# A hybrid decoder layer on one core: modulation weights transposed and summed along rows, streamed weights laid out in order of use

## The chip, the cores and the metric

One core of a Trainium2 chip runs one program, written in the Tile framework, which orders the instructions of each engine when the program is built. The metric is the device time of one execution in microseconds (us).

## The reference

One layer with two sub-layers works on x, 256 tokens by 2048 channels, in float32. All weights come from HBM, and each is used once.

```python
c_act = silu(c)                                              # c: (1, 2048)
mod = (c_act @ w_ada + b_ada).reshape(6, 2048)               # w_ada: (2048, 12288)
shift1, scale1, gate1, shift2, scale2, gate2 = mod
h = rms_norm(x, norm_g[0]) * (1 + scale1) + shift1
proj = h @ w_in                                              # w_in: (2048, 10288)
...                                                          # pooling, gated MLP and attention mixers
y = merged @ w_out                                           # merged: sigmoid gates * (mixer @ w_br_*)
x = x + gate1 * rms_norm(y, norm_g[1])
h = rms_norm(x, norm_g[2]) * (1 + scale2) + shift2
y = relu(h @ w_ff1)**2 @ w_ff2                               # 2048 -> 8192 -> 2048
x = x + gate2 * rms_norm(y, norm_g[3])
```

The product with w_ada is a matrix times one vector. It reads 100.7 MB, more than a quarter of all bytes, and does little arithmetic with them.

## The kernel before

Every large product goes through one pattern. `load_raw` issues one DMA on SP's queue for four (in the early phases two to four) k-tiles of 128 rows by 512 columns into a ring of three `raw` buffers of 1 MB. `split` makes a high part on ACT (`whi`, L183) and the rest on DVE (`wlo`, L184), two k-tiles at a time, in rings of three buffers each. `mm_a` then issues three matmuls on PE (TensorE) per k-tile and half of the tokens: high by high, low by high, high by low (L203 to L205). With 512 columns per tile of weights the DMA reads runs of 2 KB, since the weights lie in HBM row by row.

The early part runs in five phases over k (`PH`: 2, 3, 4, 3 and 4 k-tiles). In each phase twelve blocks of 512 columns of w_in are multiplied; their sums stay in PSUM or are added to SBUF by `evict`, on DVE (L396, L398). A phase can begin only when `modulate` has applied scale1 and shift1 for its k-tiles, so the modulation for phase n+1 is computed during phase n, by a Python generator that is stepped between the blocks (`step`). Behind the phases come the attention, the branch products and the gates, w_out, a normalisation, and then the feed-forward part, the longest. In all of these `fill` steps other generators (`side`) beside each 1 MB of weights: `"ada"` holds the modulation for the second sub-layer and the gates.

The modulation before has k on the partitions. `ada_gemv` loads about 1 MB of w_ada, by two DMAs for two sections of columns that lie apart or by one where they are adjacent, and multiplies it on DVE by the column `sil` of silu(c), accumulating over k-tiles into `acc` (L281, L283). What is left is a sum over the 128 partitions, which PE does. `ada_cols` needs the result per channel on the partitions: it multiplies each 128x128 piece of `acc` as stationary operand by one column of ones (L292; the trace shows two matmul records for each of these f32 matmuls), then adds the bias and the norm weight (L296 to L298). `ada_row` needs the result as a row repeated on all partitions (`gg1`, `gg2`): it splits `acc`, multiplies by `ones_r` (L313, L314) and combines with broadcast loads of b_ada and norm_g.

At the start SP's queue carries in order: c (8 KB), the identity, the first part of w_ada, the four parts of x (512 KB each), the rest of w_ada for phase 0, then w_in.

Of the kernel before, what the change touches and what calls it, by code (L numbers as in the profile page):

```python
# [13 lines left out]
P = 128  # L14
S = 256
# [30 lines left out]
V_END = 160  # L46
# [3 lines left out]
def trunk_kernel(ctx: ExitStack, tc: tile.TileContext, consts, x, c, norm_g, w_ada, b_ada, w_in,  # L50
                 pool_w, pool_scale, gmlp_ln_g, gmlp_ln_b, gmlp_ws, gmlp_bs, cmp_pos, cmp_w1,
                 cmp_b1, cmp_w2, cmp_b2, w_br_pool, w_br_gmlp, w_br_nsa, w_out, w_ff1, w_ff2, out):
# [48 lines left out]
    sil = cp.tile([P, KT], F32, name="sil")  # L101
    a_col = cp.tile([P, KT], F32, name="a_col")
    t_col = cp.tile([P, KT], F32, name="t_col")
    a2_col = cp.tile([P, KT], F32, name="a2_col")
# [8 lines left out]
    crow = pre.tile([KT, P], F32, name="crow")  # L113
    rows0 = pre.tile([96, P], F32, name="rows0")
    rows1 = pre.tile([64, P], F32, name="rows1")
    nc.sync.dma_start(crow, c.rearrange("o (r p) -> (o r) p", p=P))
# [26 lines left out]
    def load_cols():
        A.activation(ones_r, ones, AF.Copy)
        tp1 = bank("x")
        T.transpose(tp1[:, 0:V_POS + 32], rows0[0:V_POS + 32], ident[0:V_POS + 32, 0:V_POS + 32])
        T.transpose(tp1[:, V_BADA:V_END], rows1, ident[0:64, 0:64])
# [21 lines left out]
    def load_raw(src):  # L169
        k, n = src.shape[1], src.shape[2]  # L170
        raw = st.tile([P, 2048], F32, name="raw", tag="raw", bufs=3)
        v = raw[:, 0:k * n].rearrange("p (k n) -> p k n", n=n)
        nc.sync.dma_start(v, src)
        return v
# [11 lines left out]

    def kview(w):
        return w[0].rearrange("(kt p) n -> p kt n", p=P)

    win_v, wada_v = kview(w_in), kview(w_ada)  # L190
    brp_v, brg_v, brn_v = kview(w_br_pool), kview(w_br_gmlp), kview(w_br_nsa)
    wout_v, ff1_v, ff2_v = kview(w_out), kview(w_ff1), kview(w_ff2)

# [52 lines left out]
    def gemm_a_last(wv, c0, act, stores, row0=0):  # L246
# [3 lines left out]
        for u in range(0, KT, 4):  # L250
            raw = load_raw(wv[:, row0 + u:row0 + u + 4, c0:c0 + 512])
# [13 lines left out]
    def ada_gemv(c0, c1, acc):  # L265

        n = acc.shape[2]
        nk = 1024 // n
        for u in range(0, KT, nk):
            raw = ring[0].tile([P, 2048], F32, name="raw", tag="raw", bufs=ring[1])[:, 0:2 * nk * n]  # L270
            if c1 == c0 + n:
                rv = raw.rearrange("p (k s n) -> p s k n", k=nk, s=2)
                nc.sync.dma_start(raw.rearrange("p (k n) -> p k n", k=nk), wada_v[:, u:u + nk, c0:c0 + 2 * n])
            else:
                rv = raw.rearrange("p (s k n) -> p s k n", k=nk, s=2)
                for s_, c_ in enumerate((c0, c1)):
                    nc.sync.dma_start(rv[:, s_], wada_v[:, u:u + nk, c_:c_ + n])
            for k in range(nk):
                kt = u + k
                if kt == 0:  # L280
                    V.tensor_scalar(acc, rv[:, :, k], sil[:, 0:1], None, ALU.mult)  # L281
                else:
                    V.scalar_tensor_tensor(acc, rv[:, :, k], sil[:, kt:kt + 1], acc, ALU.mult, ALU.add)  # L283
            yield

    def ada_cols(k0, nk, sec, vsec, vg, a_c, t_c):

        acc = ad.tile([P, 1024], F32, name="acc", tag="acc", bufs=2)[:, 0:256 * nk]
        yield from ada_gemv(sec * D + k0 * P, (sec + 1) * D + k0 * P, acc.rearrange("p (s n) -> p s n", s=2))
# [6 lines left out]
        V.tensor_add(a_c[:, ks], ps[:, nk:2 * nk], cols[:, bs + KT:bs + KT + nk])  # L296
        V.scalar_tensor_tensor(a_c[:, ks], a_c[:, ks], 1.0, cols[:, vg + k0:vg + k0 + nk], ALU.add, ALU.mult)
        V.tensor_add(t_c[:, ks], ps[:, 0:nk], cols[:, bs:bs + nk])  # L298

    def ada_row(n, sec, gi, gg):  # L300

        acc = ad.tile([P, 1024], F32, name="acc", tag="acc", bufs=2)
        c0 = sec * D + n * 1024
        gs = gg[:, n * 1024:(n + 1) * 1024]
        nc.sync.dma_start(gs, b_ada[0, c0:c0 + 1024].partition_broadcast(P))
        yield from ada_gemv(c0, c0 + 512, acc.rearrange("p (s n) -> p s n", s=2))
        hv, lv = split(acc.rearrange("p (k n) -> p k n", k=2))
        for b in range(2):
            ps = bank("pv")
            bs = slice(b * 512, (b + 1) * 512)  # L310
            gb = ad.tile([P, 512], F32, name="gb", tag="gb", bufs=1)
            nc.sync.dma_start(gb, norm_g[0, gi, n * 1024 + b * 512:n * 1024 + (b + 1) * 512].partition_broadcast(P))
            T.matmul(ps, ones_r, hv[:, b], start=True, stop=False)  # L313
            T.matmul(ps, ones_r, lv[:, b], start=False, stop=True)  # L314
            V.tensor_add(gs[:, bs], gs[:, bs], ps)
            V.tensor_mul(gs[:, bs], gs[:, bs], gb)
# [18 lines left out]
    PH = ((0, 2), (2, 3), (5, 4), (9, 3), (12, 4))  # L335
# [37 lines left out]
    Q0, KV0, NG0, BG0 = 1536, 2560, 4096, 4144  # L373

    def part(pool, tag, bufs=1):
# [6 lines left out]
    early = [(0, pool_p, None), (512, u_p, None), (1024, v_p, None),  # L382
             (KV0, kc_p, None), (KV0 + 512, ks_p, None), (KV0 + 1024, kw_p, None),
             (Q0, flat(q32[:, 0:4]), -0.125), (Q0 + 512, flat(q32[:, 4:8]), -0.125)]
    early += [(BG0 + b * D + n * 512, dst, None) for (b, n), dst in g_p.items()]
# [3 lines left out]
    def evict(e):  # L389
        _, dst, scale = early[e]  # L390
# [297 lines left out]
    early_steps = []  # L688
    for kc in range(4):
        side["ada"][0].append(ada_cols(4 * kc, 4, 3, 2, V_G2, a2_col, t2_col))  # L690
    for ph, (k0, nk) in enumerate(PH):
# [9 lines left out]
        if ph < NP - 1:  # L701
            nxt, ns = [ada_cols(*PH[ph + 1], 0, 0, V_G0, a_col, t_col)], KT // (8 // PH[ph + 1][1])
# [3 lines left out]
        for i, e in enumerate(order):  # L706
# [7 lines left out]
            c0, _, _ = early[e]  # L714
# [3 lines left out]
            raw = load_raw(win_v[:, k0:k0 + nk, c0:c0 + 512])  # L718
# [23 lines left out]
    raw = load_raw(win_v[:, :, NG0:NG0 + 48])  # L742
# [5 lines left out]
    gT = ad.tile([48, S], F32, name="gT", tag="gb", bufs=1)  # L748
# [12 lines left out]
    def gate_chunk(b, n):  # L761
        ps = gemm(win_v, BG0 + b * D + n * 512, act)
# [39 lines left out]
    def row(n, *args):  # L802
        yield from ada_row(n, *args)
        rows.append(n)
# [192 lines left out]
```

## Time and profile before

| what | value |
|---|---|
| median of 3 runs | 1546.1 us (1539.91 to 1547.72) |
| profiled execution, own time | 1540.46 us |
| its span, first to last instruction | 1537.8 us |
| mean granted clock of PE | 0.981 |
| PE busy in the span | 1472.0 us (96%) |
| DVE busy | 1072.6 us (70%) |
| ACT busy | 764.7 us (50%) |
| moved by DMA | 368.61 MB, mean 240 GB/s |

The profile shows one execution, from its first instruction to its last; the execution's own time has 2.7 us more around it. A share of busy time is a mean over stages that differ: PE at 96% leaves 66 us of the span in which it does nothing, and a clock below 1 stretches its matmuls without making it idle. A chain of waits is read backwards from the last instruction; a row in it says what ended last at that place.

### The profile page before, as it was taken

The page shows a single profiled execution, that of the slowest core. Times are in us where ns is not written, and L with a number is a line of the kernel's source. Part 1 is how long each engine was busy: PE and PEld are TensorE (multiplying, and loading weights), DVE is VectorE, ACT ScalarE, POOL GpSimd, SP SyncE. Part 2 cuts the span into 40 slices and gives each one's busy share as a digit, 9 for nine tenths or more (in the row PEclk, how much of TensorE's full clock was granted, in tenths as well). Part 3 has the DMA queues.
Part 4 walks back from the last instruction along what each step waited for, and adds up shares of the span by engine and source line. Part 5 has one row for each costly group of instructions (what it writes and reads, how often), then busy time and mean ns, then how long its engine had stood idle before and what let it go on. Part 6 is the DMA issues. An engine that isn't in the chain of part 4 may idle for free.

```text
span 1537.8 us, 17519 instructions
## 1 busy us (share of the span) xinstructions
PE 1472.0 (96%) x6635; PEld 1193.9 (78%) x6635; DVE 1072.6 (70%) x1358; ACT 764.7 (50%) x1089; POOL 30.0 (2%) x39
## 2 busy tenths in 40 slices
PE   3989999999999999999989999999999999999997
PEld 2768877887777668787867888888888888888886
DVE  6788898778887787779887556666655445454465
ACT  5644334653677765254456453345433544344542
POOL 1000001002000010000000000000000000000000
PEclk8999998998999999999999999999999999999999
DMA  9998988665566668888975667777676555566553
GB/s 321 316 330 302 324 309 302 212 200 180 197 232 212 223 222 316 298 295 294 338 257 174 215 240 246 228 251 241 220 243 216 184 190 191 192 192 192 184 195 113
DMA packets 182339, 368.61 MB, mean 240 GB/s; under 512 B 9722, under 2 KB 22272, under 8 KB 182000
## 3 DMA queue, kind: packets, MB, share of 16 engines
q1 hardware_dynamic: 180640, 363.30, 69.8%
q0 software_dynamic: 1616, 4.20, 0.9%
q8 instruction: 52, 0.85, 0.2%
q14 instruction: 31, 0.25, 0.0%
HBM read 365.38 MB, written 2.10 MB: 239 GB/s over the span
## 4 chain that ended last, share of the span: by engine, by line
PE 83%; DVE 7%; DMA 5%; ACT 2%; issue 1%; SPq 0%; DVEq 0%; ACTq 0%
PE ps_mm L204 25%; PE ps_mm L205 25%; PE ps_mm L203 25%; DVE wlo L184 3%; DVE acc L283 2%; PE ps_x L360 2%; DMA raw<-in_w_ada_dram 2%; ACT whi L183 1%; DMA raw<-in_w_in_dram 1%; PE ps_x L292 1%; DMA raw<-in_w_out_dram 1%; PE ps_x L637 1%; PE ps_x L671 1%; DMA x_h<-in_x_dram 1%; PE ps_pv L663 1%
## 5 line engine op out<-in xcount | busy, mean ns | idle before, releaser
L184 DVE TENSOR_TENSOR wlo<-raw,whi 128x1024 fp32r<-128x1024 f32 x484 | 577.1, 1199 | 373.3 <-ACT whi L183 372.2
L183 ACT ACTIVATE whi<-raw 128x1024 fp32r<-128x1024 f32 x484 | 499.6, 1037 | 606.2 <-PE ps_mm L205 510.7
L204 PE MATMUL ps_mm<-wlo,hhi 128*128 128x512 f32 x1260 | 500.7, 397 | 9.6 <-DVE wlo L184 9.6
L203 PE MATMUL ps_mm<-whi,hhi 128*128 128x512 f32 x1260 | 497.3, 398 | 9.2 <-ACT whi L183 6.1
L205 PE MATMUL ps_mm<-whi,hlo 128*128 128x512 f32 x1260 | 498.7, 396 | 0.0
L204 PEld LDWEIGHTS ps_mm<-wlo,hhi 128*128 128x128 f32 x1260 | 239.6, 190 | 66.3 <-DVE wlo L184 16.7
L203 PEld LDWEIGHTS ps_mm<-whi,hhi 128*128 128x128 f32 x1260 | 238.5, 190 | 61.8 <-ACT whi L183 8.2
L205 PEld LDWEIGHTS ps_mm<-whi,hlo 128*128 128x128 f32 x1260 | 239.3, 190 | 51.4 <-issue 1.9
L283 DVE SCALAR_TENSOR_TENSOR acc<-raw,sil,acc 128x1024 f32<-128x1024 f32 (+2 forms) x195 | 235.2, 1206 | 7.6 <-DMA raw<-in_w_ada_dram 5.3
L203 PE MATMUL ps_mm<-whi,fhi 128*128 128x512 f32 x496 | 193.3, 390 | 0.0
L205 PE MATMUL ps_mm<-whi,flo 128*128 128x512 f32 x496 | 193.0, 389 | 0.0
L204 PE MATMUL ps_mm<-wlo,fhi 128*128 128x512 f32 x496 | 193.0, 389 | 0.0
L205 PEld LDWEIGHTS ps_mm<-whi,flo 128*128 128x128 f32 x496 | 93.1, 188 | 19.3
L204 PEld LDWEIGHTS ps_mm<-wlo,fhi 128*128 128x128 f32 x496 | 93.1, 188 | 19.3
L203 PEld LDWEIGHTS ps_mm<-whi,fhi 128*128 128x128 f32 x496 | 93.1, 188 | 19.2
L643 ACT ACTIVATE e<-e,m 128x128 f32<-128x128 f32 (+1 forms) x64 | 28.3, 443 | 1.9 <-DVE m L640 1.9
L398 DVE TENSOR_TENSOR part<-part,ps_mm 128x512 f32<-128x512 f32 x40 | 25.9, 681 | 4.4 <-PE ps_mm L205 4.4
L909 ACT ACTIVATE r_t<-ps_mm 128x512 f32<-128x512 f32 x32 | 18.8, 589 | 15.7 <-PE ps_mm L205 15.7
L403 DVE TENSOR_TENSOR pl<-ps_x,ph 128x512 fp32r<-128x512 f32 (+1 forms) x32 | 20.9, 675 | 8.1 <-ACT ph L402 8.1
L653 ACT ACTIVATE e<-e,s 128x128 f32<-128x128 f32 (+1 forms) x64 | 23.1, 441 | 5.5 <-DVE s L650 5.5
L204 PE MATMUL ps_mm<-wlo,qe 128*128 128x512 f32 x64 | 25.0, 390 | 0.0
L203 PE MATMUL ps_mm<-whi,qe 128*128 128x512 f32 x64 | 24.9, 392 | 0.0
(283 smaller groups left out, 1060.3 us busy)
## 6 DMA issues: line engine op xcount, KB each, us to landing
raw<-in_w_ff_dram SPq DMA_DIRECT2D x128, 1024.0 KB, 5.2
raw<-in_w_in_dram SPq DMA_DIRECT2D x56, 1024.0 KB, 5.3
raw<-in_w_ada_dram SPq DMA_DIRECT2D x104, 512.0 KB, 5.5
raw<-in_w_ada_dram SPq DMA_DIRECT2D x32, 1024.0 KB, 5.1
raw<-in_w_in_dram SPq DMA_DIRECT2D x24, 768.0 KB, 5.9
raw<-in_w_out_dram SPq DMA_DIRECT2D x16, 1024.0 KB, 5.3
raw<-in_w_ada_dram SPq DMA_DIRECT2D x32, 384.0 KB, 5.8
raw<-in_w_br_nsa_dram SPq DMA_DIRECT2D x8, 1024.0 KB, 5.7
```

What stands on the lines that cost most here:

```text
L183: A.activation(hv, v, AF.Copy)
L184: V.tensor_sub(lv, v, hv.bitcast(F32))
L203: T.matmul(outs[t], ahi[:, kt, ts_], hv[:, k, c0:c0 + n], start=f, stop=False, skip_group_check=True)
L204: T.matmul(outs[t], ahi[:, kt, ts_], lv[:, k, c0:c0 + n], start=False, stop=False, skip_group_check=True)
L205: T.matmul(outs[t], alo[:, kt, ts_], hv[:, k, c0:c0 + n], start=False, stop=l, skip_group_check=True)
L283: V.scalar_tensor_tensor(acc, rv[:, :, k], sil[:, kt:kt + 1], acc, ALU.mult, ALU.add)
L360: T.transpose(tb[:, (k * NT + t) * P:(k * NT + t + 1) * P], src[t][:, (k2 * 2 + k) * P:(k2 * 2 + k + 1) * P], ident)
L398: V.tensor_add(d, d, ps)
L403: V.tensor_sub(lo, src, hi.bitcast(F32))
L643: A.activation(e[:, br, 0:L], e[:, br, 0:L], AF.Exp, scale=-1.0, bias=m8[:, hh, br:br + 1], accum_out=s8[:, hh, br:br + 1])
L653: A.activation(es[hh][:, br, 0:L], es[hh][:, br, 0:L], AF.Copy, scale=s8[:, hh, br:br + 1])
L909: A.activation(r_t[:, t], ps[t], AF.Relu)
```

## The change

Two things change together.

First, the modulation. The weights come as `w_adaT`, the transpose of w_ada, so that a row holds all 2048 inputs of one output channel. `sil` becomes a 128x2048 tile: c is broadcast to all partitions by two DMAs of 512 KB, and ACT and DVE compute tanh(c/2) and (tanh + 1) * c on it. `ada_col` loads 128 rows of `w_adaT` (1 MB, one DMA, 8 KB for each partition) and one DVE instruction multiplies them by `sil`, scales by 0.5 and sums along the row into one column, `accum_out=col`. `ada_cols` calls it for shift and scale of each k-tile and then only adds bias and norm weight; nothing is left for PE. The gates are columns first (`ada_gate`, 16 calls each); `to_rows` turns them into rows in four steps by multiplying the identity with the column on DVE, splitting that, and two matmuls by `ones_r` on PE. The broadcast loads of b_ada and norm_g fall away; these vectors are transposed with the others at the start. The first gate is now first in the `"ada"` queue, and `to_rows` for it has a queue of its own, `"rows"`.

Second, the layout. All streamed weights are given to the program in another order: each block that one DMA loads is contiguous in HBM, with 8 KB (for 4 k-tiles; 4 or 6 KB in phases with 2 or 3) for each partition. The blocks, the matmuls and the splits stay as they are. The new order is made with the inputs, outside the program.

```diff
-    sil = cp.tile([P, KT], F32, name="sil")
+    sil = ad.tile([P, D], F32, name="sil")
+    for h in range(2):
+        hs = slice(h * 1024, (h + 1) * 1024)
+        nc.sync.dma_start(sil[:, hs], c[0, hs].partition_broadcast(P))
...
+    for h in range(2):
+        hs = slice(h * 1024, (h + 1) * 1024)
+        th = ring[0].tile([P, 2048], F32, name="raw", tag="raw", bufs=ring[1])[:, 0:1024]
+        A.activation(th, sil[:, hs], AF.Tanh, scale=0.5)
+        V.scalar_tensor_tensor(sil[:, hs], th, 1.0, sil[:, hs], ALU.add, ALU.mult)
...
-            raw = load_raw(wv[:, row0 + u:row0 + u + 4, c0:c0 + 512])
+            raw = load_raw(wv[c0, (row0 + u) // 4])
...
-    def ada_gemv(c0, c1, acc):
...
+    def ada_col(col, sec, k):
+
+        raw = ring[0].tile([P, 2048], F32, name="raw", tag="raw", bufs=ring[1])
+        r0 = sec * D + k * P
+        nc.sync.dma_start(raw, w_adaT[r0:r0 + P, :])
+        V.tensor_tensor_reduce(raw, raw, sil, 0.5, 0.0, ALU.mult, ALU.add, accum_out=col)
...
-        ps = bank("x")
-        for k in range(2 * nk):
-            T.matmul(ps[:, k:k + 1], acc[:, k * P:(k + 1) * P], ones[:, 0:1], start=k == 0, stop=k == 2 * nk - 1,
-                     skip_group_check=True)
+        for k in range(k0, k0 + nk):
+            for s_, c_ in enumerate((t_c, a_c)):
+                ada_col(c_[:, k:k + 1], sec + s_, k)
+                yield
...
+    def ada_gate(sec, vb, vg, g_c):
+
+        for k in range(KT):
+            ada_col(g_c[:, k:k + 1], sec, k)
+            yield
+        V.tensor_add(g_c, g_c, cols[:, vb:vb + KT])
+        V.tensor_mul(g_c, g_c, cols[:, vg:vg + KT])
+        gated.append(sec)
...
+    def to_rows(g_c, gg):
+
+        for n in range(4):
+            dh, dl = (st.tile([P, 1024], F32R, name=t, tag=t, bufs=3)[:, 0:512] for t in ("whi", "wlo"))
+            d32 = st.tile([P, 2048], F32, name="raw", tag="raw", bufs=3)[:, 0:512]
+            V.tensor_tensor(d32.rearrange("p (k n) -> p k n", k=4), ident.unsqueeze(1).broadcast_to([P, 4, P]),
+                            g_c[:, 4 * n:4 * n + 4].unsqueeze(2).broadcast_to([P, 4, P]), ALU.mult)
+            A.activation(dh, d32, AF.Copy)
+            V.tensor_sub(dl, d32, dh.bitcast(F32))
+            ps = bank("x")
+            T.matmul(ps, ones_r, dh, start=True, stop=False)
+            T.matmul(ps, ones_r, dl, start=False, stop=True)
+            A.activation(gg[:, n * 512:(n + 1) * 512], ps, AF.Copy)
+            yield
...
-            nxt, ns = [ada_cols(*PH[ph + 1], 0, 0, V_G0, a_col, t_col)], KT // (8 // PH[ph + 1][1])
+            nxt, ns = [ada_cols(*PH[ph + 1], 0, 0, V_G0, a_col, t_col)], 2 * PH[ph + 1][1]
...
-    side["ada"][0][1:1] = [row(n, 2, 1, gg1) for n in range(2)]
+    while 2 not in gated:
+        step(side["ada"][0])
+    side["rows"] = [[to_rows(g1_col, gg1)], 0.5, 0.0]
```

## Rows read from the trace of the kernel before

**Rows 1.** Page, part 1: busy time of each engine over the whole span.
```profile
PE 1472.0 (96%) x6635; PEld 1193.9 (78%) x6635; DVE 1072.6 (70%) x1358; ACT 764.7 (50%) x1089; POOL 30.0 (2%) x39
```

**Rows 2.** Windows: stretch, length, busy us (count) per engine, clock, DMA share, GB/s.
```profile
10.00:20.00 10.00, 2.62 (x10) 1.82 (x11) 7.98 (x21) 8.22 (x14) 0.00 (x0) 1.00 1.06 361
33.00:300.00 267.00, 254.49 (x1116) 206.35 (x1117) 227.09 (x269) 128.25 (x169) 6.71 (x11) 0.97 0.88 303
70.00:120.00 50.00, 44.83 (x191) 35.10 (x190) 44.00 (x50) 21.91 (x29) 0.00 (x0) 1.00 0.93 331
232.00:240.00 8.00, 8.00 (x31) 6.79 (x30) 4.19 (x9) 3.33 (x6) 0.00 (x0) 0.58 0.89 333
300.00:800.00 500.00, 489.46 (x2239) 384.94 (x2238) 403.09 (x624) 278.58 (x493) 16.79 (x11) 0.98 0.73 251
345.00:600.00 255.00, 250.44 (x1146) 188.62 (x1145) 208.59 (x407) 163.17 (x352) 15.89 (x10) 0.97 0.64 218
600.00:690.00 90.00, 86.47 (x384) 70.85 (x383) 66.88 (x65) 38.84 (x46) 0.00 (x0) 0.96 0.87 307
```

**Rows 3.** Chain that ended last, in time order: start us, duration us, what.
```profile
4.79 9.40 DMA x_h<-in_x_dram
...
28.24 1.65 PE ps_x L292 x8
...
63.90 1.25 PE ps_x L292 x12
...
120.06 1.92 PE ps_x L292 x16
...
232.31 2.23 PE ps_x L292 x16
...
397.19 1.68 PE ps_x L292 x16
```

**Rows 4.** Timeline of the start: start us, us, engine, line, operation, idle before.
```profile
24.40 0.27 PE L147 MATMUL ps_x<-cst,rows 64*128 64x64 f32 x1
...
24.99 3.10 DVE L283 SCALAR_TENSOR_TENSOR acc<-raw,sil,acc 128x512 f32<-128x512 f32 x4
...
30.36 1.09 ACT L330 ACTIVATE h<-xnT,t_col,a_col 128x256 f32<-128x256 f32 x2 [4.51 <-DVE a_col L297]
...
32.97 0.79 PE L203 MATMUL ps_mm<-whi,hhi 128*128 128x512 f32 x1 [3.10 <-ACT hhi L331]
```

**Rows 5.** Groups by shape on DVE: count, busy us, mean ns, idle before.
```profile
L283 DVE SCALAR_TENSOR_TENSOR acc<-raw,sil,acc 128x1024 f32<-128x1024 f32 x150 | 193.5, 1290 | 6.3 <-DMA raw<-in_w_ada_dram 4.8
...
L640 DVE CUSTOM_DVE_ANT_0 e<-ps_x,cst 128x256 f32<-128x256 f32 x32 | 11.8, 420 | 1.4 <-PE ps_x L637 1.3
...
L640 DVE CUSTOM_DVE_ANT_0 e<-ps_x,cst 128x128 f32<-128x128 f32 x32 | 7.8, 287 | 1.7 <-PE ps_x L637 1.5
```

**Rows 6.** Timeline of DVE during attention: start us, us, operation.
```profile
508.30 1.28 DVE L283 SCALAR_TENSOR_TENSOR acc<-raw,sil,acc 128x1024 f32<-128x1024 f32 x1
509.50 0.68 DVE L403 TENSOR_TENSOR pl<-ps_x,ph 128x512 fp32r<-128x512 f32 x1
...
516.61 0.42 DVE L640 CUSTOM_DVE_ANT_0 e<-ps_x,cst 128x256 f32<-128x256 f32 x1
...
518.33 0.42 DVE L640 CUSTOM_DVE_ANT_0 e<-ps_x,cst 128x256 f32<-128x256 f32 x1
```

**Rows 7.** Waits of PE: line, released by, total us, times, longest us.
```profile
PE ps_mm L204 <- DVE wlo L184: 9.6, 11, 2.0
PE ps_mm L203 <- ACT whi L183: 6.1, 4, 3.5
...
PE ps_pv L535 <- DVE Gt L531: 3.6, 1, 3.6
```

**Rows 8.** Chain between 200 and 260 us: start us, duration us, what.
```profile
199.91 0.23 PE ps_mm L203
...
235.17 0.43 PE ps_mm L205
```

More of the change, by code (lines that the diff above doesn't have):

```diff
@@ L45, with trunk_kernel @@
 V_BADA = 96
-V_END = 160
+V_G1, V_G3, V_BG1, V_BG2 = 160, 176, 192, 208
+V_END = 224
+Q0, KV0, NG0, BG0 = 1536, 2560, 4096, 4144
+PH = ((0, 2), (2, 3), (5, 4), (9, 3), (12, 4))
+EARLY_G = [(b, n) for n in range(2) for b in range(2)]
+LATE_G = [(b, n) for n in range(2, 4) for b in range(2)] + [(2, n) for n in range(4)]
+EARLY = [0, 512, 1024, KV0, KV0 + 512, KV0 + 1024, Q0, Q0 + 512] + [BG0 + b * D + n * 512 for b, n in EARLY_G]
+LATE = [BG0 + b * D + n * 512 for b, n in LATE_G]
 @with_exitstack
-def trunk_kernel(ctx: ExitStack, tc: tile.TileContext, consts, x, c, norm_g, w_ada, b_ada, w_in,
+def trunk_kernel(ctx: ExitStack, tc: tile.TileContext, consts, w_adaT, win_e, win_g, win_n, brp_v, brg_v, brn_v,
+                 wout_v, ff1_v, ff2_v, x, c, norm_g, b_ada,
                  pool_w, pool_scale, gmlp_ln_g, gmlp_ln_b, gmlp_ws, gmlp_bs, cmp_pos, cmp_w1,
-                 cmp_b1, cmp_w2, cmp_b2, w_br_pool, w_br_gmlp, w_br_nsa, w_out, w_ff1, w_ff2, out):
+                 cmp_b1, cmp_w2, cmp_b2, out):
     nc = tc.nc
@@ L169, in load_raw @@
     def load_raw(src):
[L170 to L174, printed above, removed]
+        n = src.shape[1]
+        raw = st.tile([P, 2048], F32, name="raw", tag="raw", bufs=3)[:, 0:n]
+        nc.sync.dma_start(raw, src)
+        return raw.rearrange("p (k n) -> p k n", n=512) if n % 512 == 0 else raw
     def split(v, store=None, ahead=150):
@@ L262, in gemm_a_last @@
         return ps
-    def ada_gemv(c0, c1, acc):
[L267 to L284, printed above, removed]
@@ L300, in ada_row @@
[L300 to L316, printed above, removed]
+        V.tensor_add(t_c[:, ks], t_c[:, ks], cols[:, bs:bs + nk])
@@ L381, in trunk_kernel @@
     g_p = {(b, n): part(gp, "gt", 4) for n in range(2) for b in range(2)}
[L382 to L385, printed above, removed]
+    early = [(dst, None) for dst in (pool_p, u_p, v_p, kc_p, ks_p, kw_p)]
+    early += [(flat(q32[:, 4 * n:4 * n + 4]), -0.125) for n in range(2)]
+    early += [(g_p[b, n], None) for b, n in EARLY_G]
     NE = len(early)
@@ L389, in evict @@
     def evict(e):
-        _, dst, scale = early[e]
+        dst, scale = early[e]
         for b, ps in enumerate(opened.pop(e)):
@@ L799, in trunk_kernel @@
     gg1 = g1p.tile([P, D], F32, name="gg1")
-    rows = []
-    def row(n, *args):
-        yield from ada_row(n, *args)
-        rows.append(n)
-    side["ada"][0][1:1] = [row(n, 2, 1, gg1) for n in range(2)]
+    while 2 not in gated:
+        step(side["ada"][0])
+    side["rows"] = [[to_rows(g1_col, gg1)], 0.5, 0.0]
     def nsa_chunk(n, gt):
-        ps = gemm(brn_v, n * 512, (yc["hi"], yc["lo"]), k_tiles=8)
+        ps = gemm(brn_v, n, (yc["hi"], yc["lo"]), k_tiles=8)
         for t in range(NT):
@@ L884, in trunk_kernel @@
     gg2 = fl.tile([P, D], F32, name="gg2")
-    for n in range(2):
-        side["ada"][0].append(ada_row(n, 5, 3, gg2))
+    side["ada"][0] += [ada_gate(5, V_BG2, V_G3, g2_col), to_rows(g2_col, gg2)]
     side["ada"][1] = 0.25
@@ L964, in _consts, with _layouts, units, phased @@
     return cst
-_INS = ['x', 'c', 'norm_g', 'w_ada', 'b_ada', 'w_in', 'pool_w', 'pool_scale', 'gmlp_ln_g', 'gmlp_ln_b',
-        'gmlp_ws', 'gmlp_bs', 'cmp_pos', 'cmp_w1', 'cmp_b1', 'cmp_w2', 'cmp_b2', 'w_br_pool', 'w_br_gmlp',
-        'w_br_nsa', 'w_out', 'w_ff1', 'w_ff2']
+def _layouts(inputs):
+    import numpy as np
+    laid = {"w_adaT": np.ascontiguousarray(inputs["w_ada"][0].T)}
+    w_in = inputs["w_in"][0]
+    def units(w, cols, k_tiles):
+        out = [w[:, c0:c0 + 512].reshape(-1, k_tiles, P, 512).transpose(0, 2, 1, 3) for c0 in cols]
+        return np.ascontiguousarray(np.stack(out)).reshape(len(cols), -1, P, k_tiles * 512)
+    def phased(c0):
+        parts = [w_in[k0 * P:(k0 + nk) * P, c0:c0 + 512].reshape(nk, P, 512).transpose(1, 0, 2) for k0, nk in PH]
+        return np.concatenate([p.ravel() for p in parts])
+    laid["win_e"] = np.stack([phased(c0) for c0 in EARLY])
+    laid["win_g"] = units(w_in, LATE, 4)
+    laid["win_n"] = np.ascontiguousarray(w_in[:, NG0:NG0 + 48].reshape(KT, P, 48).transpose(1, 0, 2)).reshape(P, KT * 48)
+    for name in ("w_br_pool", "w_br_gmlp", "w_br_nsa", "w_out", "w_ff1", "w_ff2"):
+        w = inputs[name][0]
+        laid[name] = units(w, range(0, w.shape[1], 512), 4)
+    return laid
+_INS = ['x', 'c', 'norm_g', 'b_ada', 'pool_w', 'pool_scale', 'gmlp_ln_g', 'gmlp_ln_b',
+        'gmlp_ws', 'gmlp_bs', 'cmp_pos', 'cmp_w1', 'cmp_b1', 'cmp_w2', 'cmp_b2']
 _OUTS = [((1, 256, 2048), 'float32')]
```

67 lines of the change are left out of this document (30 added, 37 removed).

## The prediction

> **What bounds the kernel now.** I read the page first, then windows, the waits of PE, the chain by time, and the shapes on DVE. PE works in 1472.0 of 1537.8 us [rows 1], so only two things can shorten the end: less work on PE, or less of the 66 us in which it idles (and of the time in which its clock is low). The page's average hides where these lie. In the feed-forward part PE never waits; nothing but matmuls counts there, and the change leaves those alone. The idle time lies in the start, where the first weight matmul comes at 32.97 us [rows 4], in the early phases (12.5 us of PE's time from 33 to 300) and up to the second normalisation (10.5 from 300 to 800) [rows 2]. In a window of 50 us with much of it PE has 44.83, DVE 44.00 and the DMA engines a share of 0.93 [rows 2]: three resources at their limit together, so that relief of one alone gives little. Attention (345 to 600 us) is PE's again, 250.44 of 255 us, with DVE at 82% behind it [rows 2]. The waits say the same: matmuls wait most for `wlo` on DVE, then for `whi`, which itself mostly waited for a transfer, and once 3.6 us for `Gt` on DVE [rows 7].
>
> **The change part by part.** All terms stand against the profiled execution, 1540.5 us.
>
> *PE loses L292.* In the early phases this is four runs on the chain: 1.25 us for a phase of three k-tiles, which occurs twice, and 1.92 and 2.23 us for one of four [rows 3]: 1.25 x 2 + 1.92 + 2.23 = 6.65 us. In the attention and behind it are four more runs of 16 matmuls, each 1.68 us as in the one shown [rows 3]: 6.7 us. The second sum lies where PE is the bound, so it counts in full. The first counts in full only if DVE and the transfers let PE go ahead by as much; I take it whole because DVE gets lighter there too (next but one), with 0 as the other end. The 1.65 us of phase 0 are in the start's own sum. `to_rows` issues 16 matmuls of 512 columns where `ada_row` issued 16: no difference.
>
> *The start.* Two broadcasts of c, 1.05 MB together, go on SP's queue ahead of everything. At the 361 GB/s of that stretch [rows 2] they delay each later transfer by 2.9 us: the last part of x from 14.2 us [rows 3] to 17.1, the transposes of x and behind them L147 on PE from 24.4 [rows 4] to 27.3, and the last of phase 0's w_ada likewise. What follows that gets shorter. Before, four accumulations ended at 28.09 [rows 4], L292 took 1.65 us, then `h` began at 30.36 [rows 4]. After, `cols` is ready about 0.5 us behind L147, at 28.1, and the last row-sum should be over by then: its data come about 24, and it takes 2.2 us. Two small DVE steps, some 0.3 us, and `h` can begin at 28.4, if ACT, whose copies of x are late by the same 2.9 us, is free. 30.36 - 28.4 = 2.0 us gained. The ends: 5 us gained if the tile scheduler orders L147 sooner, 3 us lost if the broadcast lands on the critical path in full and nothing gets shorter. The new tanh and multiply on 2048 columns are hidden by the wait for x: they need c alone, which is first in the queue.
>
> *DVE.* The trace has no multiply-and-sum over 2048 columns. It has the same custom operation at 128 and 256 columns, 287 and 420 ns [rows 5], or 1.04 ns per column, and six of them back to back begin 0.34 us apart (516.61 is the first, 518.33 the sixth), read-out of the accumulator included [rows 6]. So 2048 columns should occupy DVE for 0.34 + 1792 x 1.04 ns = 2.21 us. Before, 1 MB took two instructions of 1290 ns [rows 5]; with other work between them each holds DVE for 1.20 us [rows 6], in a row the second waits for the sum of the first. That is 2.4 to 2.6 us. For about 33 MB of w_ada in the early part DVE saves 0.2 to 0.4 us each, 7 to 13 us. What PE gets of it is bounded by the 12.5 us in which it idles from 33 to 300 [rows 2]. I take 3 us, the low end, because SP, `evict` and the splits stay as they are and one late transfer still stops PE. The ends are 0 and 12.5.
>
> *The clock.* Behind L292's 16 one-column matmuls at 232.31 us, and two short waits before them, matmuls come 0.43 us apart [rows 8] instead of the usual 0.23 [rows 8], and the granted clock is 0.58 from 232 to 240 [rows 2]: the lower level. About 6 us at half pace cost 3 us. With L292 gone I take 2 us of that back; 0 if waits remain there.
>
> *The layout.* Bytes stay the same but for some 3 MB of broadcasts. SP issues one DMA for 1 MB of w_ada instead of two. Runs of 8 KB may move faster than 2 KB, and nothing in the trace prices that: no stretch has runs of 8 KB alone. The worth lies between 0, if the transfers go on as now, and the waits of PE that start at a late transfer. The largest of those is the 3.5 us `whi` wait [rows 7] in the stretch from 600 to 690, whose clock of 0.96 costs as much again [rows 2]. I take 3 us, nearer to nothing, since in most places the slots of the ring and not the rate say when a transfer starts.
> The Trainium skill ("DMA: Bandwidth & Descriptors", "Why small descriptors are slow") puts a fixed cost of about 3 cycles on each packet; by that, as an estimate, 64 beats of 32 B for 2 KB would cost 67 cycles and 8 KB 259 for 256, a gain of 3.4%. No run here shows it yet.
>
> *What gets worse.* A row-sum holds DVE for 2.2 us without a break. Before, other work could come between the halves, as `pl` does at 509.50 us, right behind an accumulation [rows 6]. So a split or a `pl` can come 1.0 us later than before, where DVE was in the middle. The rings of three hide this wherever PE has two tiles ahead. `to_rows` also takes a `raw` buffer for each of its steps, so SP has one load less in flight there. I charge 2 us for both, with 0 and 10 as ends.
>
> Sum: -6.7 - 6.7 - 2.0 - 3 - 2 - 3 + 2 = -21.4, or 1519 us for an execution like the profiled one. The median of the runs shown is 5.6 us above that execution and the lowest run just below it. I put the forecast a little above the sum, 1522 us.
>
> **The rivals.**
>
> *Little comes out.* PE's relief in the early part is given back, because the transfers there set the pace (share 0.93 [rows 2]) and the layout doesn't speed them; the start is no earlier. Only the four later runs of L292 and some 1 us remain: 1540.5 - 8 = 1533 by the profiled one, and around 1538 by the median. For it: three resources at their limit together. Against: DVE does get lighter, and PE does wait for DVE more than for anything [rows 7].
> The Trainium skill (same page, "Specifications") gives about 358 GB/s as what HBM yields for one core; by that rule the layout could gain nothing where 331 to 361 GB/s are already moved. The trace agrees only in part: 361 GB/s were measured in a stretch [rows 2].
>
> *More comes out.* Transfers get markedly faster, and with lighter DVE nearly all waits of PE between 33 and 800 us go, 12.5 + 10.5 us [rows 2], and 2 us of clock: 1540.5 - 13.4 - 2 - 25 = 1500 us. For it: each wait begins at DVE or at a transfer. Against: the ring's slots, and queues that other work fills.
>
> *Slower, by blocking on DVE.* There are 76 row-sums between the start and the feed-forward part. If each makes something wait 1.0 us more and PE has no tile in hand, that is up to 76 us, where DVE is busiest. It decides for slower by more than 0.5% when the waits of some 29 of the 76 reach PE (21.4 + 7.7 us). With half of them: 1540.5 - 23.4 + 38 = 1555 us. Against: PE waits now only 9.6 us for `wlo` in all [rows 7], although two accumulations in a row hold DVE for 2.6 us already.
>
> *Row-sums at half pace.* The rows that price them read one source from PSUM; with two in SBUF the operation might need two cycles per column, 4.3 us. That would be 2.1 x 33 = 69 us more on DVE from 33 to 300, where 39.9 us of it are free [rows 2]: PE pays 30 at the least, and DVE's own gain of 3 is gone. 1540.5 - 18.4 + 30 = 1552 us. Two-source instructions from SBUF at one column per cycle, as the accumulations are [rows 5], speak against it.
>
> **How the numbers follow.** Chances: the forecast 0.58, little 0.17, more 0.13, blocking 0.08, half pace 0.04. The range from 1500 to 1546 leaves out both slower cases and half of "more", 0.18. A measurement of this kernel can tell some 0.5%, 7.7 us, from no change. Faster by over 0.5%: 0.55 of the forecast, all of "more", a little of "little": 0.70. Within: 0.17. Slower: 0.13.
>
> **What would show it.** L292 gone and the first L203 near 31 us; row-sums near 2.3 us; the clock at 232 to 240 at full level; `wlo` waits of PE below 9.6 us in all; DMA share below 0.93 in the early part at equal GB/s. I am wrong if row-sums take over 3 us, if `pl` or `wlo` waits of PE grow by over 10 us, or if the early phases end no sooner than before.

## The result and the profile after

| | kernel before | changed kernel |
|---|---|---|
| median, same chip, alternating (4 runs each) | 1543.01 us (1538.42 to 1547.72) | 1518.28 us (1517.32 to 1520.20) |
| ratio | | 0.9852, interval 0.9827 to 0.9877 |
| profiled execution, own time | 1540.46 us | 1517.32 us |
| its span | 1537.8 us | 1515.1 us |
| mean granted clock of PE | 0.981 | 0.989 |

The changed kernel is 1.2 to 1.7% faster. The forecast was 1522 us, so its size is met too. The page of the changed kernel, the busy times and the group of the row-sum:

```profile
PE 1448.4 (96%) x6507; PEld 1171.8 (77%) x6507; DVE 1052.0 (69%) x1341; ACT 771.0 (51%) x1102; POOL 36.4 (2%) x43
...
L283 DVE CUSTOM_DVE_ANT_0 raw<-raw,sil 128x2048 f32<-128x2048 f32 x96 | 219.2, 2286 | 7.8 <-DMA raw<-in_w_adaT_dram 7.6
```

Against [rows 1] PE is busy 23.6 us less, with the 128 records of L292 gone. Its idle time, span less busy, was 65.8 us and is 66.7 us. So the whole gain lies in the time in which PE is busy, its stretching by a low clock included, and none in what it waits for; DVE's 20.6 us less came with no less idle time on PE. The same stretches as in [rows 2], of the changed kernel:

```profile
33.00:300.00 267.00, 252.79 (x1088) 203.64 (x1089) 228.38 (x273) 133.33 (x174) 7.62 (x12) 0.98 0.82 307
70.00:120.00 50.00, 45.11 (x190) 34.72 (x189) 45.35 (x55) 22.50 (x31) 0.00 (x0) 1.00 0.88 341
232.00:240.00 8.00, 6.46 (x28) 4.69 (x26) 8.00 (x9) 2.33 (x3) 0.00 (x0) 1.00 0.99 384
300.00:800.00 500.00, 481.93 (x2208) 377.25 (x2207) 407.06 (x653) 292.33 (x524) 20.39 (x10) 0.99 0.68 247
345.00:600.00 255.00, 251.88 (x1156) 188.96 (x1154) 210.13 (x406) 170.11 (x358) 20.39 (x10) 1.00 0.65 237
```

Read the last three columns first. From 33 to 300 us the DMA engines are busy 0.82 of the time instead of 0.88 and yet move 307 GB/s instead of 303: 374 GB/s at a full share against 344. From 232 to 240 us the clock is 1.00, where it was 0.58. PE's busy time from 33 to 300 has gone down by 1.7 us, though: it idles for 14.2 us there where it was 12.5. (The stretch from 300 to 800 now holds a wait of 9.2 us at the second normalisation that before came behind 800.) The waits of PE:

```profile
PE ps_mm L217 <- DVE wlo L204: 13.6, 16, 3.0
...
PE ps_mm L216 <- ACT hhi L336: 6.0, 1, 6.0
...
PE ps_mm L216 <- ACT whi L203: 2.9, 3, 1.6
PE ps_pv L537 <- DVE Gt L533: 1.7, 1, 1.7
```

Against [rows 7], `whi` has fallen from 6.1 to 2.9 us and `Gt` from 3.6 to 1.7, but `wlo` has risen from 9.6 to 13.6 (what that means is taken up with the next kernels). Landmarks of the two traces (us from the start):

| | first weight matmul | first matmul of the gates behind the phases | first score matmul | first square behind w_out | feed-forward, first and last relu |
|---|---|---|---|---|---|
| before | 33.0 | 332.8 | 407.7 | 732.2 | 836.4, 1441.4 |
| changed | 33.7 | 326.5 | 394.4 | 710.6 | 814.7, 1419.3 |

The start is 0.7 us later, the phases give 7.0 us, the part from there to the first square 15.3 us more. The feed-forward part has the same length, 605 us from the first relu to the last.

One more reading helps, because one execution of a kernel differs from the next by several us. Each run comes with its span and its mean granted clock. Span x (1 - clock) is taken here as the time that the lower clock costs, and the rest as the length at full clock. In 65 runs of the kernel before the time goes from 1532.67 to 1551.62 us and the clock from 0.988 to 0.975, so much of that spread is clock. Means over all runs of each kernel (the experiments are explained below):

| kernel | runs | at full clock, us | cost of the clock, us |
|---|---|---|---|
| before | 65 | 1512.0 | 26.3 |
| changed (two measurements) | 9 | 1497.9 | 20.1 |
| new layout alone | 12 | 1509.0 | 27.7 |
| new modulation alone (two measurements) | 10 | 1502.2 | 21.0 |
| before with one matmul for each of L292's groups | 6 | 1502.5 | 18.0 |
| the same and the new layout | 6 | 1501.7 | 17.2 |
| changed, L292's matmuls put back | 11 | 1508.9 | 24.5 |
| changed, columns first | 5 | 1502.5 | 17.0 |
| changed, columns in the middle | 6 | 1503.7 | 15.7 |
| changed, half sums, new tile | 12 | 1519.0 | 20.8 |
| changed, half sums, no new tile | 9 | 1508.6 | 22.5 |
| changed, 64 B more in SBUF | 6 | 1510.0 | 19.6 |

Runs of one kernel scatter by 1 to 2.6 us about the third column (standard deviation); the clock is listed to 0.001, which is 1.5 us in one run. The change gave 14.1 us at full clock and 6.2 us through the clock.

### The profile page after: what moved, and what is told of

Its sections match the earlier page's. It is cut to its first block, busy times and chain, and to the rows that moved or that the text cites. A ratio compares the mean times of both kernels' runs of the same rounds, so it can differ in the third digit from the quotient of the medians.

```text
span 1515.1 us, 17069 instructions
## 1 busy us (share of the span) xinstructions
PE 1448.4 (96%) x6507; PEld 1171.8 (77%) x6507; DVE 1052.0 (69%) x1341; ACT 771.0 (51%) x1102; POOL 36.4 (2%) x43
## 4 chain that ended last, share of the span: by engine, by line
PE 84%; DVE 9%; ACT 3%; DMA 2%; issue 2%; POOL 0%; DVEq 0%; ACTq 0%; POOLq 0%
PE ps_mm L217 26%; PE ps_mm L218 26%; PE ps_mm L216 25%; DVE raw L283 3%; DVE wlo L204 3%; PE ps_x L364 2%; ACT whi L203 1%; PE ps_x L639 1%; PE ps_x L673 1%; PE ps_pv L665 1%; PE ps_pv L664 1%; DVE part L400 0%; PE ps_x L638 0%; DMA raw<-in_w_out_dram 0%; DMA cst<-consts_dram 0%
## 5 line engine op out<-in xcount | busy, mean ns | idle before, releaser
L204 DVE TENSOR_TENSOR wlo<-raw,whi 128x1024 fp32r<-128x1024 f32 x484 | 576.1, 1199 | 373.5 <-ACT whi L203 372.4
L283 DVE CUSTOM_DVE_ANT_0 raw<-raw,sil 128x2048 f32<-128x2048 f32 x96 | 219.2, 2286 | 7.8 <-DMA raw<-in_w_adaT_dram 7.6
L905 ACT ACTIVATE r_t<-ps_mm 128x512 f32<-128x512 f32 x32 | 18.8, 588 | 15.7 <-PE ps_mm L218 15.7
L364 PE MATMUL ps_x<-cst,x_h 128*128 128x128 f32 x32 | 6.8, 365 | 20.2 <-DVE x_h L355 15.4
```

The source lines that it names most:

```text
L204: V.tensor_sub(lv, v, hv.bitcast(F32))
L283: V.tensor_tensor_reduce(raw, raw, sil, 0.5, 0.0, ALU.mult, ALU.add, accum_out=col)
L364: T.transpose(tb[:, (k * NT + t) * P:(k * NT + t + 1) * P], src[t][:, (k2 * 2 + k) * P:(k2 * 2 + k + 1) * P], ident)
L905: A.activation(r_t[:, t], ps[t], AF.Relu)
```

## The experiments

Theory A, from the prediction: L292 was most of it, by its own time on PE, with small gains from DVE, the start and the layout. Rival B: the transfers were most of it. Rival C: row-sums that hold DVE for long give part of the gain back. The kernels ran in four groups, each on another chip and beside runs of the kernel before there, and each ratio is against these: layout alone, modulation alone, L292 alone and L292's matmuls put back; columns first, half sums with a new tile and the changed kernel again; columns in the middle, half sums without a new tile and the shift; the second measurement of the modulation and L292 with the new layout.

### The two halves, and L292 by itself

*Layout alone.* The kernel before, with the weights in the new order. `ada_gemv` stays, and w_ada is loaded in its old order. One of the loads, the others likewise:

```diff
...
-            raw = load_raw(wv[:, row0 + u:row0 + u + 4, c0:c0 + 512])
+            raw = load_raw(wv[c0, (row0 + u) // 4])
...
```

> The kernel before with only the layout of the streamed weights changed (w_ada and its sums as before). If the gain comes mostly from PE's lost matmuls, as the sum had it, the layout gives some 5 us (0.997 of before, 0.994 to 1.000), mainly between 600 and 690 us. If it comes mostly from faster transfers, 15 us or more (0.990 or lower), with the early phases ending sooner by 5 us or more. The bytes per busy share of the DMA engines should be higher than before either way.

Measured: 1539.69 us against 1539.73, ratio 0.999 (0.9969 to 1.0011). The windows of this kernel, early phases:

```profile
33.00:300.00 267.00, 252.35 (x1112) 204.78 (x1112) 226.72 (x268) 128.06 (x170) 6.71 (x11) 0.97 0.85 302
```

The DMA engines do the same work with less: share 0.85 instead of 0.88 for 302 GB/s. PE gets next to nothing of it here: its idle time is 65.0 us instead of 65.8. Rival B falls.

*Modulation alone.* The changed kernel with `load_raw` reading the old order, the inverse of the diff above. The 8 KB rows of `w_adaT` belong to this half.

> The changed kernel with the streamed weights in their old layout: only the modulation changes. By the sum, 15 to 18 us faster than before (0.988 to 0.990). If the transfers are the main cause, 7 us or less (0.995 or above), because the waits for transfers in the early part come back.

Measured: 1523.68 us, ratio 0.9896 (0.9874 to 0.9919). A second measurement:

> The modulation alone once more, for a closer figure of what the layout adds to it. If the layout adds 3 us or more to the new modulation, this stays at 0.989 to 0.990 of before against 0.985 to 0.987 of the changed kernel. If the layout adds nothing, it comes out at 0.986 to 0.987.

Measured: 1526.70 us, ratio 0.9917 (0.9888 to 0.9947). The modulation by itself carries most of the gain, 13 to 16 us by the medians. The second ratio is above both cases of its expectation (its interval takes in the first): with the new modulation the layout is worth some 7 us by the mean ratios (0.9907 and 0.9859), where with the old one it was worth 1.5 (0.999). The early phases of the first measurement:

```profile
33.00:300.00 267.00, 252.76 (x1085) 203.44 (x1086) 227.94 (x273) 133.46 (x175) 7.62 (x12) 0.97 0.84 306
```

At a full share that is 364 GB/s, against 344 before, 355 with the layout alone and 374 with both.

*L292 alone.* The kernel before, with one matmul of up to eight columns where each group had up to eight matmuls of one. The sums of all but the first 128 channels of a group are left out; 18 of the 128 records stay.

```diff
-        for k in range(2 * nk):
-            T.matmul(ps[:, k:k + 1], acc[:, k * P:(k + 1) * P], ones[:, 0:1], start=k == 0, stop=k == 2 * nk - 1,
-                     skip_group_check=True)
+        T.matmul(ps[:, 0:2 * nk], acc[:, 0:P], ones[:, 0:2 * nk], start=True, stop=True)
```

> The kernel before with one matmul by ones in place of 2*nk for each group (L292): the sums of all but the first 128 channels of a group are left out, their columns hold the first's. DVE and the transfers stay. If time on PE is what L292 costs, 120 of its 128 records go and with them some 11 to 13 us (0.992 to 0.993). If the early part is held by DVE and transfers and gives PE's relief back, only the four later groups count: 6 to 7 us (0.996).

Measured: 1521.48 us, ratio 0.9893 (0.9869 to 0.9916). All of `ada_gemv`, all splits and all transfers are those of before, and the time is that of the new modulation. The window in which the clock was low:

```profile
232.00:240.00 8.00, 6.99 (x30) 5.67 (x31) 8.00 (x10) 4.06 (x6) 0.00 (x0) 1.00 0.96 341
```

The clock is 1.00 where [rows 2] had 0.58. L292 alone is worth 16.5 us by its ratio (0.0107 of 1540), and by the table 9.5 at full clock and 8.3 through the clock; the 11 to 13 us that were expected were PE's own time. This kernel, whose DVE work is that of before, also has the longer waits for `wlo`:

```profile
PE ps_mm L204 <- DVE wlo L184: 13.5, 16, 1.7
```

So the rise from 9.6 to 13.6 us in the changed kernel is no sign of its long row-sums: it is there without them, once PE has less to do.

*L292 alone with the new layout.* Both edits of this section in the kernel before.

> The kernel before with the new layout of the streamed weights and one matmul by ones for each group in place of 2*nk (the other sums are left out). The two parts that seem to count, without the new modulation's row-sums. If these two are the whole gain, the time is that of the changed kernel, 0.985 to 0.987 of before. If the row-sums on DVE give a share of their own, it stays at 0.990 to 0.992. If the layout is worth nothing even without L292, it equals the earlier run with one matmul by ones, 0.989.

Measured: 1521.79 us, ratio 0.9887 (0.9856 to 0.9919). The same as without the layout, within the intervals; this interval takes in the changed kernel's ratios as well, so it can't tell whether the row-sums have a share of their own.

*L292's matmuls put back.* The changed kernel with as many matmuls of one column, from the identity, in `ada_cols`.

```diff
+        ps = bank("x")
+        for k in range(2 * nk):
+            T.matmul(ps[:, k:k + 1], ident, ones[:, 0:1], start=k == 0, stop=k == 2 * nk - 1, skip_group_check=True)
```

> The changed kernel with L292's matmuls issued again, from the identity and without use of their result. If PE's time is the price, 13 to 15 us slower than the changed kernel (0.994 to 0.995 of before). If the early part hides them, 7 us slower (0.990).

Measured: 1535.87 us, ratio 0.9977 (0.9963 to 0.9992). That is 14.5 us more than the changed kernel in its second measurement (below) by the medians and 17 by the ratios, each against the kernel before on its own chip; the ratio is above the 0.994 to 0.995 expected. The place isn't that of before, since these matmuls wait for nothing: those of all early phases came first on PE. The chain of this kernel:

```profile
27.62 1.07 PE ps_x L293 x8
28.73 10.21 PE ps_x L293 x56
38.95 0.64 PE ps_mm L216
```

And the windows before, under and behind them:

```profile
24.00:28.70 4.70, 4.41 (x29) 3.06 (x27) 1.11 (x3) 4.05 (x7) 0.00 (x0) 1.00 0.96 377
28.70:38.90 10.20, 10.16 (x57) 10.17 (x57) 10.19 (x12) 3.62 (x5) 0.00 (x0) 0.61 0.67 247
38.90:44.00 5.10, 5.10 (x13) 4.01 (x13) 0.13 (x2) 0.60 (x1) 0.00 (x0) 0.50 0.64 258
```

PE is busy all the time under them, and yet the granted clock falls from 1.00 to 0.61, and to 0.50, the lower level, behind them; 56 records took 10.2 us, 0.18 us each, where the shortest run of 16 in [rows 3] took 0.105 us each. So the sum is confirmed, the split over places is not.

### The start

The start had become later, so it was looked at by itself. Timeline of the changed kernel (start, duration, instruction, idle time before it):

```profile
27.45 0.24 PE L167 MATMUL ps_x<-cst,rows 64*128 64x64 f32 x1
...
27.73 0.23 DVE L168 COPY cols<-ps_x 128x71 f32<-128x71 f32 x1 [3.85 <-PE ps_x L167]
...
28.07 2.28 DVE L283 CUSTOM_DVE_ANT_0 raw<-raw,sil 128x2048 f32<-128x2048 f32 x1
...
30.48 1.23 DVE L204 TENSOR_TENSOR wlo<-raw,whi 128x1024 fp32r<-128x1024 f32 x1
31.62 0.16 DVE L294 SCALAR_TENSOR_TENSOR a_col<-a_col,cols 128x2 f32<-128x2 f32 x1
...
31.87 1.09 ACT L335 ACTIVATE h<-xnT,t_col,a_col 128x256 f32<-128x256 f32 x2 [3.29 <-DVE a_col L294]
...
33.68 0.79 PE L216 MATMUL ps_mm<-whi,hhi 128*128 128x512 f32 x1 [5.99 <-ACT hhi L336]
```

DVE stands idle for 3.85 us at the copies into `cols`, which wait for transposes that PE does behind all of x. The fourth row-sum is queued behind those copies and begins at 28.07 us, and a split of w_in (L204) stands between it and the last step for `a_col`. Two kernels move `load_cols`.

*Columns first*, ahead of the transposes of x:

```diff
+    load_cols()
...
-    load_cols()
```

> The changed kernel with the transposes of the bias and norm vectors (load_cols) issued ahead of the transposes of x, so that DVE no longer waits for L167 in front of the fourth row-sum. If that order is why the start gained nothing, the first weight matmul comes at 29 to 31 us instead of 33.7, and the whole is 3 to 4 us shorter than the changed kernel (0.983 of before). If the transfers of phase 0 hold it, the first matmul stays past 33 us, or it comes sooner and the end doesn't move.

*Columns in the middle*, in the loop over x, behind its third part:

```diff
+        if k2 == 2:
+            load_cols()
...
-    load_cols()
```

> The changed kernel with load_cols issued between the transposes of x (behind the third pair), so that DVE copies the bias and norm columns before the third row-sum is over and the fourth starts as its data land. If DVE's order was what cost the start its gain, the first weight matmul comes at 30 to 31.5 us instead of 33.7 to 34.4, and the end moves by 2 to 3 us (0.984 of before). If the first matmul moves and the end doesn't, the early phases are held by something else, transfers or DVE.

*The changed kernel again*, on the same chip as the first of these:

> The changed kernel as it is, beside the others on the same chip: 0.985 of before.

Measured: columns first 1521.66 us, ratio 0.9870 (0.9841 to 0.9899); columns in the middle 1522.08 us, 0.9878 (0.9856 to 0.9899); the changed kernel again 1521.37 us, 0.9866 (0.9836 to 0.9897). No gain from either; the first weight matmul comes at 33.7 and 33.9 us, not at the 29 to 31.5 expected. Waits of PE with the columns first:

```profile
PE ps_x L165 <- DMA rows<-in_cmp_pos_dram: 10.2, 1, 10.2
...
PE ps_x L166 <- DMA rows<-in_b_ada_dram: 3.9, 1, 3.9
```

Now PE stands before small transfers that come late, and the transposes of x stand behind them. In the middle, the fourth row-sum is early, but the timeline shows what is next:

```profile
24.50 2.28 DVE L283 CUSTOM_DVE_ANT_0 raw<-raw,sil 128x2048 f32<-128x2048 f32 x1
...
27.02 0.16 DVE L294 SCALAR_TENSOR_TENSOR a_col<-a_col,cols 128x2 f32<-128x2 f32 x1
...
30.64 0.60 ACT L370 ACTIVATE xnT<-ps_x 128x512 f32<-128x512 f32 x1 [0.35 <-PE ps_x L364]
31.13 1.05 ACT L203 ACTIVATE whi<-raw 128x1024 fp32r<-128x1024 f32 x1
32.07 1.08 ACT L335 ACTIVATE h<-xnT,t_col,a_col 128x256 f32<-128x256 f32 x2
```

The last step for the column begins 4.6 us sooner (27.02 instead of 31.62), and `h` begins at 32.07 instead of 31.87: ACT's copies of x and a split stand ahead of it. The order of DVE was one bound of the start, with a second right behind it.

### Long row-sums on DVE

The place where the changed kernel waits longest for `wlo`, in its timeline:

```profile
236.51 2.29 DVE L283 CUSTOM_DVE_ANT_0 raw<-raw,sil 128x2048 f32<-128x2048 f32 x1
...
238.72 2.29 DVE L283 CUSTOM_DVE_ANT_0 raw<-raw,sil 128x2048 f32<-128x2048 f32 x1
...
240.93 1.83 DVE L204 TENSOR_TENSOR wlo<-raw,whi 128x1024 fp32r<-128x1024 f32 x2
...
242.22 0.50 PE L217 MATMUL ps_mm<-wlo,hhi 128*128 128x512 f32 x1 [2.98 <-DVE wlo L204]
```

Two row-sums in a row hold DVE for 4.4 us, and the split that PE needs stands behind them. The granted clock then falls, as the windows show:

```profile
236.00:242.00 6.00, 3.23 (x15) 2.33 (x13) 6.00 (x7) 0.92 (x2) 0.39 (x1) 1.00 1.01 423
242.00:247.00 5.00, 4.79 (x14) 3.80 (x15) 5.00 (x7) 3.30 (x5) 2.76 (x5) 0.66 0.79 275
```

So the low stretch that L292 had at 232 us has partly come back, ten us later, behind a stall of PE. The same wait, 2.96 us, stands at 243.5 us in the second profile of the changed kernel and in that of the new modulation alone; in the latter the clock is 1.00 from 240 to 270 us, so a fall does not follow each time.

To see what the length of a row-sum costs in all, each was cut in two halves with an addition.

*Half sums, with a new tile for the second half:*

```diff
-        V.tensor_tensor_reduce(raw, raw, sil, 0.5, 0.0, ALU.mult, ALU.add, accum_out=col)
+        c2 = ad.tile([P, 1], F32, name="c2", tag="c2", bufs=2)
+        for hs, dst in ((slice(0, 1024), col), (slice(1024, 2048), c2)):
+            V.tensor_tensor_reduce(raw[:, hs], raw[:, hs], sil[:, hs], 0.5, 0.0, ALU.mult, ALU.add, accum_out=dst)
+        V.tensor_add(col, col, c2)
```

> The changed kernel with each row-sum cut into two of 1024 columns and an addition of the halves: DVE is busy for some 25 us more in all, but free in between. If blocking by one long instruction costs PE, the waits of PE for wlo fall from 13.6 to below 10 us and the time falls by 2 us or more. If DVE's load is what counts, PE waits more, and the time rises by 3 to 10 us. If neither, it is the same as the changed kernel's within 0.25%.

Measured: 1541.37 us, ratio 1.0003 (0.9980 to 1.0026), 20 us more than the changed kernel. The feed-forward part alone had become 7.6 us longer, although PE doesn't wait there: it is busy all the time, and the last row-sums end in it at about 1130 us in the changed kernel. The new tile shifts what lies behind it in SBUF, so the next two kernels separate the halves from the shift.

*Half sums without a new tile:* the second half goes into columns of `cols` that nothing uses.

```diff
-        V.tensor_tensor_reduce(raw, raw, sil, 0.5, 0.0, ALU.mult, ALU.add, accum_out=col)
+        i = V_POS + 32 + k
+        for hs, dst in ((slice(0, 1024), col), (slice(1024, 2048), cols[:, i:i + 1])):
+            V.tensor_tensor_reduce(raw[:, hs], raw[:, hs], sil[:, hs], 0.5, 0.0, ALU.mult, ALU.add, accum_out=dst)
+        V.tensor_add(col, col, cols[:, i:i + 1])
```

> The half sums again, with the second half's result in unused columns of an existing tile, so that no other tile changes its place in SBUF. If the place was behind the slower matmuls of the last products, these are back at 226.7 ns apart and the stage behind 860 us is as long as in the changed kernel (some 8 us regained); what is left, some 10 us over the changed kernel, is the price of 25 us more on DVE. If it is DVE's work that slows them, the matmuls stay at 233 ns.

*The shift without halves:* the changed kernel and a tile of 64 B per partition behind `sil` that nothing reads.

```diff
+    pad = ad.tile([P, 16], F32, name="pad")
+    G.memset(pad, 0.0)
```

> The changed kernel with an unused tile of 64 B per partition behind sil, which shifts all later tiles on that side by 64 B. If place in SBUF sets the pace of the last products, their matmuls are 233 ns apart instead of 226.7 and the whole is 7 to 10 us slower than the changed kernel (0.991 of before). If not, it is equal to the changed kernel (0.985 to 0.987).

Measured: half sums without a new tile 1533.12 us, ratio 0.9943 (0.9917 to 0.9969); the shift alone 1531.68 us, ratio 0.9941 (0.9921 to 0.9962). Each costs some 10 to 12 us against the changed kernel (0.9866), and the two together make the 20 us. The halves, in the page of the kernel without the new tile, and its waits:

```profile
L285 DVE CUSTOM_DVE_ANT_0 raw<-raw,sil 128x1024 f32<-128x1024 f32 x192 | 232.2, 1232 | 9.3 <-DMA raw<-in_w_adaT_dram 9.2
...
PE ps_mm L217 <- DVE wlo L204: 13.7, 21, 1.3
...
PE ps_mm L216 <- ACT whi L203: 7.9, 7, 4.4
```

With read-outs and additions DVE has 1071.6 us of work instead of 1052.0, and PE's idle time goes from 66.7 to 74.8 us. The longest wait for `wlo` falls from 3.0 to 1.3 us, but their sum stays at 13.7 where below 10 would have shown a price of blocking, and the waits for `whi` rise from 2.9 to 7.9 us. Shorter instructions don't help in total: with 20 us more on DVE the kernel is some 11 us longer. Its feed-forward part is back at 604.6 us. The matmuls of w_ff2 in the changed kernel's timeline, and then in that of the kernel with 64 B more (the first and the ninth):

```profile
1299.78 0.39 PE L216 MATMUL ps_mm<-whi,fhi 128*128 128x512 f32 x1
...
1301.60 0.39 PE L218 MATMUL ps_mm<-whi,flo 128*128 128x512 f32 x1
```

```profile
1299.72 0.39 PE L219 MATMUL ps_mm<-wlo,fhi 128*128 128x512 f32 x1
...
1301.59 0.39 PE L218 MATMUL ps_mm<-whi,fhi 128*128 128x512 f32 x1
```

Eight steps take 1.82 us in the one and 1.87 us in the other; over 40 us it is 226.6 ns a matmul against 233.4. The clock is 1.00 in both. From the first relu to the last the feed-forward part takes 612 us instead of 605, and from there to the end, with the last products of w_ff2, it is 98.7 us instead of 95.8: 10.5 us together, nearly all that the shift costs.

## Why the prediction was right

*PE loses L292: right, and the bulk.* The text had 6.65 + 6.7 us, and 1.65 us in the sum of the start: 15.0 us. Taking 110 of L292's 128 records away, and nothing else, gave 16.5 us, putting its matmuls back cost 14.5 to 17. Both hold clock besides: by the table 9.5 us at full clock and 8.3 through the clock for the first, 11.0 and 4.4 for the second. In the trace the part from the gates to the first square, where 6.7 us were due, gave 15.3 us in the first profile and 8.8 in the second one, whose clock costs there what it cost before; in the first, 8.5 of the 15.3 us are clock (next point).

*The clock: right in place and sign, too small.* 2 us were taken for one stretch, 232 to 240 us, which came back to 1.00. Over all runs the clock gives 6.2 us. Its cost moves from one execution to the next: in the changed kernel's two profiled executions, from 330 to 700 us, it is 1.7 and 10.2 us (summed over windows of 10 us), against 10.2 in that of before.

*The start: wrong in sign, the step that failed.* The text let the fourth row-sum be over when `cols` is ready, "its data come about 24", and let `h` begin at 28.4 us. The data were no obstacle (with the columns in the middle this row-sum ran at 24.50 us); DVE's order was. The copies into `cols` stand ahead of the fourth row-sum in DVE's queue, they wait for PE to finish x, and so 2.3 us of row-sum come after `cols` and not before; the 1.2 us of the split behind it, which the text didn't count, come on top. `h` began at 31.87 us, the first weight matmul came 0.7 us later than before instead of 2.0 us earlier. The bound that the text gave, 3 us lost, holds it, but for another reason than the one named there.

*DVE: the price right, the worth not found.* 2.21 us were worked out for a row-sum, 2.286 us were measured, and DVE lost 20.6 us of work, at the low end of 0.2 to 0.4 us for each MB. Of the 3 us that PE should get nothing shows: its idle time is 66.7 us (64.7 in the second profile), and the new modulation alone is no shorter at full clock than the kernel before with L292 reduced to one matmul, 1502.2 against 1502.5 us. In the early part, where the 3 us were put, the traces show a loss against the kernel with L292 alone reduced: the first matmul of the gates comes at 321.5 us there and at 323.3 with the layout as well, but at 326.3 to 327.7 in all seven traces of the new modulation with whole row-sums and without L292's matmuls. The later start is 1.0 to 2.4 us of that, and the clock is another part: from 30 to 330 us it costs 2.4 and 3.0 us in the first two and 3.4 to 8.5 in the seven. The half sums show that DVE's time does matter to PE.

*The layout: about the size, near what can be told.* 3 us were taken. At full clock the new order gives 2.4 us in the kernel before (against the runs of its own chip; 3.0 by the table), 0.8 us with L292 reduced, and 4.3 us on top of the new modulation, each to about 1 us. In the time itself only the last is seen, and there the intervals of the ratios (0.9852 and 0.9866 with it, 0.9896 and 0.9917 without) lie close to each other or overlap. That transfers need less of the engines is shown: from 33 to 300 us the layout alone moves 3% more at a full share (355 against 344 GB/s), near the 3.4% that the prediction estimated, and both halves together 9% (374). How much of it PE gets, between 0 and some 4 us at full clock, stays open.

*Blocking: named, its price not found.* 2 us were charged. `wlo` waits are 13.6 us where the text wanted them below 9.6, but they are 13.5 with L292 alone reduced and 13.7 with half sums, so their sum doesn't price long row-sums. What these bring is the single long wait, 3.0 us at 242 where the longest is 1.7 with the old accumulations. `whi` and `Gt` fell by 5.1 us together.

*The rivals.* "Little comes out" was right that PE's idle time would stay as it was, but it let PE's 6.65 us in the early phases be given back, and the phases gave 7.0. "More" needed the idle time to go. "Slower, by blocking" needed 29 of 76 row-sums to reach PE with 1.0 us each; all `wlo` waits are 16. "Half pace" fell with 2.286 us for a row-sum.

So the sum came out because its largest part was right. L292 and its clock are 17.0 of the 21.4 us in the text (6.65 + 6.7 + 1.65 + 2) and gave 16.5 us by the ratio, 17.8 by the table, where the whole change gave 20.3 by the table and 20.6 and 22.8 by its two ratios. The other terms, 4.4 us in the text, come to 2.5 us by the table and 4 to 6 by the ratios; one of them has the wrong sign and the others can't be told apart, so that their sum comes near is partly luck. A kernel that only did L292's work in fewer matmuls would have had most of the gain, as far as these runs show; its remaining sums were left out here.

## What to carry to other kernels

Where PE is the bound, count its short work first, down to matmuls of one column: here it cost its own time and, in the mean over the runs, 8 us through the clock, and it could be tried alone by one edit. Relief on an engine or a queue off the path is worth only what falls in PE's idle time, so compare span less busy before and after; here it did not move. A sum of waits that grows is not yet a price of the change: look whether it also grows in a kernel without the suspected cause. When a step is to start earlier, write down the order of its engine's queue up to it, for what stands ahead of it there, waiting for something else, decides.

## What was not expected of the hardware

*Placement in SBUF changes the pace of matmuls.* 64 B more per partition behind `sil` made the matmuls of w_ff2 come 233.4 ns apart instead of 226.6, at a granted clock of 1.00 and with no wait: 7.6 us up to the last relu and 2.9 behind it, of the some 10 to 12 us that this kernel is longer. Why is not shown. In the kernels of the first section of experiments the feed-forward part is 605 us, as in the kernel before, so they are not touched by it there. So an experiment that adds a tile measures its place too.

*The clock fell under one-column matmuls that followed each other without a pause.* At 28.7 to 38.9 us of the kernel with L292's matmuls put back PE was busy 10.16 of 10.20 us, and the granted clock was 0.61, after 1.00 in the 4.7 us before; in the 5.1 us of weight matmuls behind them it was 0.50, the lower level.

*The rate of transfers.* In the changed kernel 384 GB/s were moved from 232 to 240 us, where before 333 were [rows 2], and 423 from 236 to 242. The limit of about 358 GB/s that a rival's sentence in the prediction took from the Trainium skill ("DMA: Bandwidth & Descriptors", "Specifications") is thus passed. The Trainium skill ("HBM Reference", "Specifications (TRN2)") says itself that a core that streams alone gets well above that share; the trace agrees, with the 384 and 423 GB/s above.
